# Moving the weight buffers of a one-core transformer block by 64 bytes, and spacing the gated MLP's activations 1040 bytes apart

## The chip, the core and the metric

The kernel runs on one core of a Trainium2 chip. The metric is the device time of one execution in microseconds (us); shorter is better. Three runs of the kernel before gave 1280.26, 1278.90 and 1280.11 us, median 1280.11.

## What is computed

One layer of a hybrid encoder block on a sequence of 256 tokens of width 2048, in float32:

```
mod = silu(c) @ W_ada + b_ada                  -> shift1, scale1, gate1, shift2, scale2, gate2
h   = RMSNorm(x) * (1 + scale1) + shift1
P   = h @ W_in                                 2048 -> 7184 columns
      group A: 4 heads x 256, bidirectional mLSTM;  group B: 8 heads x 128, 2-D neighbourhood attention
x   = x + gate1 * (concat[A, B] @ W_out)       2048 -> 2048
h   = RMSNorm(x) * (1 + scale2) + shift2
u, g = split(h @ W_up)                         2048 -> 2 x 5632
x   = x + gate2 * ((gelu(conv3(g)) * u) @ W_down)      5632 -> 2048
out = RMSNorm(x)
```

## The kernel before

Activations lie transposed: 128 features on the partitions, 256 tokens along the row. Every weight matrix is streamed once from HBM in pieces of 128 partitions x 1024 floats (4096 bytes a partition, tile `wr`; `wre` is two further buffers of it that serve only early on). float32 precision is had by splitting each operand in a high and a low part: ScalarE (ACT) casts `wr` to the high part `wh` (L356), VectorE (DVE) subtracts to get the low part `wl` (L364), and TensorE (PE) runs three matmuls for each 128x128 block of weights (`mm_w`, L391 to L393): high activation by high weight, low by high, high by low. In each, the activation row of 256 tokens is the moving operand (streamed through the array) and a 512-byte slice of `wh` or `wl` is the stationary one (loaded beforehand; the profile shows the loads as a row of its own, PEld). For the value projections (`mm_x`, L398 to L400) the sides change: 512 weight columns move and 128 tokens of an activation are loaded.

Stages in order of time:

- **Projections** (tile `acc`): 14 column chunks, five groups of K, with the modulation, the mLSTM and the attention beside them.
- **Output projection** (tile `acc_r`, activations `hh`/`hl`).
- **Up projection** (tile `acc_u`, `second_half`): 22 chunks of 512 columns x 16 K tiles x 4 column blocks x 3 matmuls = 4224 matmuls on `hh`/`hl`.
- **Down projection** (tile `acc_r` again, through `rows`): 44 K tiles x 16 column blocks x 3 = 2112 matmuls. The first 40 K tiles (j = 0 to 39) come from `aTh` and `aTl`, the last four from `hh`/`hl`.

The order of issue on every engine is fixed when the program is built, by a small model of the engines' times; addresses play no part in it.

What the change touches is where tiles lie. A pool lays its tiles one after another along the partition's row, in the order of first use, and pools follow each other: `cpool` (constants, `xT`), `ring` (`hh`, `hl`: 16 buffers of 1024 bytes each), `wpool` (`wr`, `h_t`, `wh`, `wl`, then `ared`, a tile of 16 bytes that takes 64, then `ar`), and after them, once the first half is over, `upool` (`aTh`, `aTl`, `g_c`). The start addresses within a partition that follow, and their place within 512 bytes, the size of a weight slice:

```
tile      before    mod 512     after    mod 512    step from buffer to buffer, before / after
hh         45568        0       45568        0      1024 / 1024
hl         61952        0       61952        0      1024 / 1024
wr         78336        0       78400       64      4096 / 4096
wh         97792        0       97856       64      4096 / 4096
wl        110080        0      110144       64      4096 / 4096
ar        122432       64      122496      128      4096 / 4096
aTh[0]    138816       64      138880      128      1024 / 1040
aTl[0]    179776       64      180480      256      1024 / 1040
wre       204640      352      204704      416      4096 / 4096
```

So before the change `hh` and `hl` stand at the same place within 512 bytes as every weight slice, and `aTh` and `aTl` stand 64 bytes past it, because of `ared`.

Of the kernel before, what the change touches and what calls it, by code (L numbers as in the profile page):

```python
# [7 lines left out]
F32 = mybir.dt.float32  # L8
F32R = mybir.dt.float32r
# [5 lines left out]
P = 128  # L15
D = 2048
KT = D // P
S = 256
# [8 lines left out]
FT = FF // P  # L27
# [40 lines left out]
N_LATE = 2.0  # L68
SEEDS = (0, 1, 1, 1, 1)
CH = 512  # L70
PIECE = 1024

CHUNK_COLS = {}
# [14 lines left out]
def splits(n, step):  # L88
    return [(a, min(a + step, n)) for a in range(0, n, step)]


def group_bounds():
    out, k = [], 0
    for g in KGROUPS:
        out.append((k, k + g))
        k += g
    return out
# [6 lines left out]
def up_order():  # L104
    return [(kind, c) for c in range(FF // CH) for kind in "gu"]

# [36 lines left out]
def block_kernel(ctx, tc, xT_d, cols_d, bg_d, rpb_d, ada_d, win_d, wg_d, wout_d, wup_d, wdown_d, const_d, out_d):  # L143
# [4 lines left out]
    cpool = ctx.enter_context(tc.tile_pool(name="cpool", bufs=1))  # L148
    ring = ctx.enter_context(tc.tile_pool(name="ring", bufs=1))
    wpool = ctx.enter_context(tc.tile_pool(name="wpool", bufs=1))  # L150
    psk = ctx.enter_context(tc.tile_pool(name="psk", bufs=2, space=PSUM))

    A.preload_act_table_set("natural_log_exp_and_others")
# [13 lines left out]
    def col(name):  # L167
        a, b = NCOL[name]
        return cols[:, a:b]

# [1 line left out]
    class Sched:  # L172
        LAT = {"PE": 0.2, "DVE": 0.14, "ACT": 0.14, "SP": 0.0, "POOL": 0.0}

# [69 lines left out]
    def held(what):  # L244
        return any(a in flags and b not in flags and what in c for a, b, c in HOLDS)
# [4 lines left out]
    def dve(n, *conds):  # L250
        return "DVE", 0.07 + n / 960, conds

    def act(n, *conds):
        return "ACT", 0.1 + n / 1210, conds
# [22 lines left out]
    class Ring:  # L277
# [12 lines left out]
        def take(self):  # L290
# [3 lines left out]
            if e:  # L294
                t = pools["e"].tile([P, PIECE], F32, name=self.tag + "e", tag=self.tag + "e", bufs=self.ne)
            else:
                t = wpool.tile([P, PIECE], F32, name=self.tag, tag=self.tag, bufs=self.n)
            return t, slots
# [19 lines left out]
        hl = ring.tile([P, S], F32R, name="hl", tag="hl", bufs=HH_BUFS)  # L318
        return hh, hl

# [1 line left out]
    class Stream:  # L322
        def __init__(self):
            self.todo, self.raw, self.cut, self.half = [], {}, {}, {}
# [4 lines left out]
        def add(self, src, nk):  # L329
            a = self.at.get(id(src), 0)  # L330
            self.at[id(src)] = a + P * nk * CH
            self.todo.append((src, a, nk))

        def view(self, t, nk):
            return t[:, : nk * CH].rearrange("p (a b) -> p a b", a=nk)

# [5 lines left out]
        def fetch(self, i, t):  # L342
            src, a, nk = self.todo[i]
            raw, slots = self.wr.take()
            n = nk * CH
            nc.sync.dma_start(raw[:, :n], src[a : a + P * n].rearrange("(p n) -> p n", p=P))
            self.raw[i] = (raw, sch.dma(t, n), slots)

        def cutting(self):
            for i, (_, _, nk) in enumerate(self.todo):  # L350
                n = nk * CH
                t = yield act(n, lambda: self.raw[i][1] if i in self.raw else None, self.wh.has())
                self.wh.take()
                raw = self.view(self.raw[i][0], nk)
                wh = self.view(wpool.tile([P, PIECE], F32R, name="wh", tag="wh", bufs=WH_BUFS), nk)
                A.copy(wh, raw)  # L356
                self.half[i] = (raw, wh, t)

        def rest(self):
            for i, (_, _, nk) in enumerate(self.todo):  # L360
                t = yield dve(nk * CH, lambda: self.half[i][2] if i in self.half and not held("r") else None)
                raw, wh, _ = self.half.pop(i)
                wl = self.view(wpool.tile([P, PIECE], F32R, name="wl", tag="wl", bufs=WH_BUFS), nk)
                V.tensor_sub(wl, raw, wh.bitcast(F32))  # L364
# [20 lines left out]
    stream = Stream()  # L385
# [50 lines left out]
        out[k] = (hh, hl)  # L436
        flags["h", part, k] = t

# [1 line left out]
    class Ada:  # L440
        def __init__(self):
            self.seq = ada_seq()
# [17 lines left out]
        def fetch(self, q, n, raw, slots, t):  # L460
            a = n * P * PIECE
            q.dma_start(raw, ada_d[a : a + P * PIECE].rearrange("(p n) -> p n", p=P))  # L462
            self.raw[n] = (raw, sch.dma(t, PIECE), slots)
# [145 lines left out]
    V.memset(ones, 1.0)  # L609
    V.memset(eps, EPS)  # L610

# [1 line left out]
    def silu():  # L613
        c = col("c")
        warm = kb.take()
        for i in range(WARM):
            T.matmul(warm[:, :P], ones, ones, start=i == 0, stop=i == WARM - 1)
        kb.give(5.3)
        sch.clock["PE"] = 1.1 + 0.215 * 2 * WARM
        yield act(16, lambda: 3.3)  # L620
        A.activation(small, c, AF.Exp, scale=-1.0)
        yield dve(1)
        V.tensor_scalar(small, small, 1.0, None, ALU.add)
        yield dve(100)
        V.reciprocal(small, small)
        t = yield dve(16)
        V.tensor_mul(sc, small, c)
        flags["sc"] = t
        diag = res["qb"].rearrange("p a b -> p (a b)")
        for q in range(4):  # L630
            d = diag[:, q * 512 : (q + 1) * 512]
            t = yield dve(512)
            V.tensor_tensor(d.rearrange("p (a b) -> p a b", a=4), ident.unsqueeze(1).to_broadcast([P, 4, P]),
                            sc[:, 4 * q : 4 * q + 4].unsqueeze(2).to_broadcast([P, 4, P]), ALU.mult)
            sch.add(srow_part(q, d), -2, t)

    def srow_part(q, d):
        yield pe(0.87, pb.has())
        tp = pb.take()
        T.matmul(tp, ones, d, start=True, stop=True)  # L640
        t = yield copy(512)
        put(srow[:, q * 512 : (q + 1) * 512], tp)
        pb.give(t)
        flags["srow", q] = t

# [1 line left out]
    ssb = {}  # L647

    n1_sums = KT - len(N1_PAIRS)
# [45 lines left out]

    mix = [None] * KT

# [1 line left out]
    nraw, nsl, npt = Slots(2), Slots(2), Slots(2)  # L699

    def natten(heads):
# [57 lines left out]
            mix[8 + h] = (hh, hl)  # L759
            flags["mix", 8 + h] = t  # L760

# [1 line left out]
    gst = {}  # L763
    mhs, mes = Slots(2), Slots(4)

# [243 lines left out]
            A.activation(o, o, AF.Exp, scale=-1.0)  # L1009
            flags["sig", i] = t  # L1010

# [1 line left out]
    bounds = group_bounds()  # L1013
    hT = [None] * KT

# [82 lines left out]
        stream.add(wout_d, (n1 - n0) * P * nk // CH)  # L1098
    at_up = len(stream.todo)

# [1 line left out]
    ss2 = {}  # L1102

    def wout_close(acc, c, n0, n1):
# [34 lines left out]
    order = up_order()  # L1139
# [4 lines left out]
    for _, n0, n1, _, nk in down_steps():  # L1144
        stream.add(wdown_d, (n1 - n0) * P * nk // CH)

# [1 line left out]
    for what in FIRST_LOADS:  # L1148
        if what == "x":
            a = 4 * len(xhere)  # L1150
# [7 lines left out]
            spare = spare.rearrange("p a b c -> p (a b c)" if len(spare.shape) == 4 else "p a b -> p (a b)")  # L1158
            ada.fetch(nc.sync, n, spare[:, n % 2 * PIECE : (n % 2 + 1) * PIECE], Slots(0), 0.0)

# [1 line left out]
    starts = [len(CHUNK_ORDER) * sum(len(splits(q1 - q0, 2)) for q0, q1 in bounds[:g]) for g in range(len(bounds))]  # L1162

    def pace(p):
# [23 lines left out]
    A.preload_act_table_set("gelu_and_others")  # L1188
    pstack.close()

# [1 line left out]
    upool = ctx.enter_context(tc.tile_pool(name="upool", bufs=1))  # L1192
    accu = ctx.enter_context(tc.tile_pool(name="accu", bufs=3, space=PSUM))
    aslots, gslots = Slots(3), Slots(GC_BUFS)
    h2 = [None] * KT
    n_own = FT - CH // P
    aTh = upool.tile([P, n_own, S], F32R, name="aTh")
    aTl = upool.tile([P, n_own, S], F32R, name="aTl")
    aT = [(aTh[:, j, :], aTl[:, j, :]) for j in range(n_own)] + [None] * (FT - n_own)
    cw0, cb0 = NCOL["cw"][0], NCOL["cb"][0]  # L1200
    gated = {}

# [35 lines left out]
        gslots.give(t)  # L1238
        flags["a", j] = t

# [1 line left out]
    ss3 = {}  # L1242
    gf0 = NCOL["gf"][0]

# [183 lines left out]
```

## Time and profile before

| what | value |
|---|---|
| median of the runs | 1280.11 us (1278.90 to 1280.26) |
| profiled execution, first to last instruction | 1278.2 us |
| PE busy | 1253.4 us, 98% |
| DVE, ACT, POOL busy | 908.2, 680.4, 110.6 us |
| moved by DMA | 322.55 MB, mean 252 GB/s |
| projections / output projection | from 19.4 us / from 395 us |
| up / down projection | from 504 us / 1014 to 1264 us |

The profile's own time for its execution is its span, 1278.2 us; the runs' times are the device's and lie 0.7 to 2.1 us above it. A matmul's own duration (0.28 us) is longer than the distance from its start to the next one's start, since matmuls overlap in the array; what sets the time is the distance between starts.

### The profile page before, as it was taken

To read this page: it belongs to the slowest core of one execution; us is meant where nothing else is said; L and a number is where in the kernel's file an instruction comes from. 1 tells how busy PE (TensorE), PEld (TensorE's weight loads), DVE (VectorE), ACT (ScalarE), POOL (GpSimd) and SP (SyncE) were. 2 spreads that over 40 slices of the span, in tenths; PEclk is the share of its full clock that TensorE was granted. 3 is DMA by queue.
4 is the path that set the end of the run, shared out by engine and by line. 5 is a ranking of instruction groups with operands and counts; after the bars stand their busy time and mean duration, and the time that the engine had idled before them with its cause. 6 is when DMAs were issued, how large, how long until landed. Compare 5 with 4: busy or idle time off the path is not lost.

```text
span 1278.2 us, 24381 instructions
## 1 busy us (share of the span) xinstructions
PE 1253.4 (98%) x9822; PEld 1217.2 (95%) x9822; DVE 908.2 (71%) x1382; ACT 680.4 (53%) x1027; POOL 110.6 (9%) x208
## 2 busy tenths in 40 slices
PE   8999999999999998999999999999999999999996
PEld 6889999999989998999999999999999999999995
DVE  5998879889999997997666666666665645454543
ACT  5986667668767444554444444444443534343442
POOL 1111111123112111010000000000000000000000
PEclk8999999999999998999999999999999999999998
DMA  9999889988888996786667666666655555655552
GB/s 322 408 370 352 298 297 374 338 285 292 298 297 277 376 330 244 263 323 235 217 215 228 217 216 215 224 224 220 202 184 183 182 183 184 193 183 186 185 182 91
DMA packets 91313, 322.55 MB, mean 252 GB/s; under 512 B 10560, under 2 KB 11072, under 8 KB 91200
## 3 DMA queue, kind: packets, MB, share of 16 engines
q1 hardware_dynamic: 63360, 220.84, 50.4%
q0 software_dynamic: 27840, 100.15, 23.3%
q8 instruction: 77, 1.26, 0.4%
q14 instruction: 36, 0.29, 0.1%
HBM read 318.85 MB, written 2.10 MB: 251 GB/s over the span
## 4 chain that ended last, share of the span: by engine, by line
PE 95%; ACT 3%; DVE 1%; DMA 1%; issue 0%; DVEq 0%; POOL 0%
PE acc_u L392 13%; PE acc_u L393 13%; PE acc_u L391 13%; PE acc_r L391 9%; PE acc_r L393 9%; PE acc_r L392 9%; PE acc L391 6%; PE acc L392 6%; PE acc L393 6%; PE acc L398 2%; PE acc L399 2%; PE acc L400 2%; ACT wh L356 1%; PE bank L890 1%; DMA n_raw<-in_rpb 1%; PE bank L850 1%
## 5 line engine op out<-in xcount | busy, mean ns | idle before, releaser
L364 DVE TENSOR_TENSOR wl<-wr,wh 128x1024 fp32r<-128x1024 f32 (+1 forms) x391 | 466.4, 1193 | 292.0 <-ACT wh L356 290.3
L356 ACT CAST wh<-wr 128x1024 fp32r<-128x1024 f32 (+1 forms) x391 | 400.4, 1024 | 467.1 <-PE acc_u L392 221.0
L391 PE MATMUL acc_u<-hh,wh 128*128 128x256 f32 x1408 | 399.8, 284 | 3.4 <-ACT hh L432 3.4
L392 PE MATMUL acc_u<-hl,wh 128*128 128x256 f32 x1408 | 399.7, 284 | 0.1
L393 PE MATMUL acc_u<-hh,wl 128*128 128x256 f32 x1408 | 399.5, 284 | 0.0
L391 PEld LDWEIGHTS acc_u<-hh,wh 128*128 128x128 f32 x1408 | 271.5, 193 | 3.9 <-ACT hh L432 3.9
L392 PEld LDWEIGHTS acc_u<-hl,wh 128*128 128x128 f32 x1408 | 271.5, 193 | 0.4 <-DVE hl L434 0.4
L393 PEld LDWEIGHTS acc_u<-hh,wl 128*128 128x128 f32 x1408 | 271.5, 193 | 0.0
L391 PE MATMUL acc<-hh,wh 128*128 128x256 f32 x640 | 186.8, 292 | 4.6 <-ACT hh L432 2.3
L392 PE MATMUL acc<-hl,wh 128*128 128x256 f32 x640 | 182.2, 285 | 0.0
L393 PE MATMUL acc<-hh,wl 128*128 128x256 f32 x640 | 182.0, 284 | 0.0
L391 PE MATMUL acc_r<-aTh,wh 128*128 128x256 f32 x640 | 179.7, 281 | 0.0
L392 PE MATMUL acc_r<-aTl,wh 128*128 128x256 f32 x640 | 178.6, 279 | 0.0
L393 PE MATMUL acc_r<-aTh,wl 128*128 128x256 f32 x640 | 178.6, 279 | 0.0
L462 POOL DMA_DIRECT2D ar<-in_ada x173 | 91.7, 531 | 716.4 <-DVE modp L489 352.5
L391 PEld LDWEIGHTS acc<-hh,wh 128*128 128x128 f32 x640 | 123.5, 193 | 10.0 <-ACT acc L260 3.6
L392 PEld LDWEIGHTS acc<-hl,wh 128*128 128x128 f32 x640 | 123.6, 193 | 1.0 <-DVE are L457 0.2
L393 PEld LDWEIGHTS acc<-hh,wl 128*128 128x128 f32 x640 | 123.6, 193 | 0.0
L393 PEld LDWEIGHTS acc_r<-aTh,wl 128*128 128x128 f32 x640 | 120.2, 188 | 0.0
L391 PEld LDWEIGHTS acc_r<-aTh,wh 128*128 128x128 f32 x640 | 120.1, 188 | 0.1
L392 PEld LDWEIGHTS acc_r<-aTl,wh 128*128 128x128 f32 x640 | 119.8, 187 | 0.1
L489 DVE CUSTOM_DVE_ANT_0 ar<-ar,srow,modp 128x1024 f32<-128x1024 f32 x87 | 111.1, 1277 | 0.6 <-DMA ar<-in_ada 0.3
(202 smaller groups left out, 1572.1 us busy)
## 6 DMA issues: line engine op xcount, KB each, us to landing
wr<-in_wup SPq DMA_DIRECT2D x176, 512.0 KB, 3.6
ar<-in_ada POOLq DMA_DIRECT2D x173, 512.0 KB, 5.6
wr<-in_wdown SPq DMA_DIRECT2D x88, 512.0 KB, 4.1
wr<-in_win SPq DMA_DIRECT2D x73, 512.0 KB, 5.7
wr<-in_wout SPq DMA_DIRECT2D x32, 512.0 KB, 5.8
wre<-in_win SPq DMA_DIRECT2D x25, 512.0 KB, 5.4
are<-in_ada POOLq DMA_DIRECT2D x15, 512.0 KB, 5.8
wr<-in_win SPq DMA_DIRECT2D x22, 256.0 KB, 5.4
```

The source lines that it names most:

```text
L356: A.copy(wh, raw)
L364: V.tensor_sub(wl, raw, wh.bitcast(F32))
L391: T.matmul(acc[:, n, :], w_h, h[0], start=st, stop=False, skip_group_check=True)
L392: T.matmul(acc[:, n, :], w_h, h[1], start=False, stop=False, skip_group_check=True)
L393: T.matmul(acc[:, n, :], w_l, h[0], start=False, stop=last, skip_group_check=True)
L398: T.matmul(acc[:, t, :], h_h, wh[:, k, :], start=first, stop=False, skip_group_check=True)
L399: T.matmul(acc[:, t, :], h_h, wl[:, k, :], start=False, stop=False, skip_group_check=True)
L400: T.matmul(acc[:, t, :], h_l, wh[:, k, :], start=False, stop=last, skip_group_check=True)
L462: q.dma_start(raw, ada_d[a : a + P * PIECE].rearrange("(p n) -> p n", p=P))
L489: V.tensor_tensor_reduce(raw, raw, srow[:, h * PIECE : (h + 1) * PIECE], 1.0, modp[:, part, k : k + 1] if h else cols[:, c : c + 1], ALU.m ...
L850: T.matmul(sp[:, u * S : (u + 1) * S], kT[:, 2 * h + k, u * P : (u + 1) * P], qT[:, 2 * h + k, :], start=k == 0, stop=k == 1)
L890: T.matmul(nu[1][:, : DH_A + 1], at[d][:, j, :], va[:, u, h, :], start=n == 0, stop=n == len(blocks) - 1)
```

## The change

Two constants are added. `SHIFT = 16` floats is an unused tile of 64 bytes a partition at the head of `wpool`, so that all of `wpool` and all that lies behind it stands 64 bytes further on, while `cpool` and `ring` stay. `STEP = 4` floats lengthens each row of `aTh` and `aTl` from 1024 to 1040 bytes; the last 16 bytes are not used. No instruction, no order and no wait differs on any engine; addresses do. (The diff also empties comment lines, left out here.)

```diff
 CH = 512
+SHIFT = 16
+STEP = 4
 PIECE = 1024
...
     wpool = ctx.enter_context(tc.tile_pool(name="wpool", bufs=1))
+    wpool.tile([P, SHIFT], F32, name="shift", tag="shift")
     psk = ctx.enter_context(tc.tile_pool(name="psk", bufs=2, space=PSUM))
...
     n_own = FT - CH // P
-    aTh = upool.tile([P, n_own, S], F32R, name="aTh")
-    aTl = upool.tile([P, n_own, S], F32R, name="aTl")
-    aT = [(aTh[:, j, :], aTl[:, j, :]) for j in range(n_own)] + [None] * (FT - n_own)
+    aTh = upool.tile([P, n_own, S + STEP], F32R, name="aTh")
+    aTl = upool.tile([P, n_own, S + STEP], F32R, name="aTl")
+    aT = [(aTh[:, j, :S], aTl[:, j, :S]) for j in range(n_own)] + [None] * (FT - n_own)
```

## The prediction

> **What bounds the kernel now.** I read the page first, then busy time by stage, then single matmuls.
>
> ```profile
> span 1278.2 us, 24381 instructions
> ...
> PE 1253.4 (98%) x9822; PEld 1217.2 (95%) x9822; DVE 908.2 (71%) x1382; ACT 680.4 (53%) x1027; POOL 110.6 (9%) x208
> ```
>
> PE is busy for all but 25 us of the span. By stage (length, busy time and count of each engine, granted clock, DMA share, GB/s):
>
> ```profile
> 0.00:100.00 100.00, 92.79 (x606) 80.44 (x607) 83.86 (x149) 77.73 (x137) 16.69 (x35) 0.97 0.97 367
> 100.00:200.00 100.00, 100.00 (x707) 93.91 (x706) 85.29 (x115) 67.60 (x100) 13.73 (x26) 1.00 0.90 316
> ...
> 395.00:498.00 103.00, 102.52 (x826) 101.08 (x825) 92.78 (x154) 48.65 (x75) 18.85 (x35) 1.00 0.93 331
> ...
> 520.00:1000.00 480.00, 480.00 (x4003) 480.00 (x4001) 323.76 (x433) 224.32 (x302) 19.53 (x37) 1.00 0.68 224
> 1014.00:1260.00 246.00, 246.00 (x2083) 245.84 (x2082) 117.65 (x119) 101.28 (x118) 0.00 (x0) 1.00 0.56 178
> ```
>
> From 100 us on PE has no gap to speak of, at full clock, and in the up and down projections the others have room. The two engines that feed it wait for it to free a weight buffer (us in total, times, longest):
>
> ```profile
> ACT wh L356 <- PE acc_u L392: 221.0, 142, 5.0
> ACT wh L356 <- PE acc_r L392: 182.0, 106, 3.5
> ```
>
> So the time is a count of matmuls times the distance between their starts, and that distance is not the same in the two last stages. A matmul takes 0.28 us, so a window also counts those begun 0.28 us before it: up 480.28/4003 = 120.0 ns, down 246.28/2083 = 118.2 ns, for the same instruction at the same clock. One place of the down projection shows both, where K tile 43 (`hh`, `hl`) gives way to K tile 0 of the next chunk (`aTh`, `aTl`). Timeline of PE: start, length, instruction.
>
> ```profile
> 1074.78 0.28 PE L391 MATMUL acc_r<-hh,wh 128*128 128x256 f32 x1
> ...
> 1076.22 0.28 PE L391 MATMUL acc_r<-aTh,wh 128*128 128x256 f32 x1
> ...
> 1081.88 0.28 PE L391 MATMUL acc_r<-aTh,wh 128*128 128x256 f32 x1
> ```
>
> Three matmuls a block, four blocks a K tile: 12 intervals on `hh` take 1.44 us, 120.0 ns each; the 48 on `aTh` take 5.66 us, 117.9 ns each. Same stage, same weight buffers, same shape; only the activations' place differs, level with the weight slice within 512 bytes for `hh`, 64 bytes past it for `aTh`. The load of the next weights starts together with each matmul (all engines' timeline):
>
> ```profile
> 1076.22 0.28 PE L391 MATMUL acc_r<-aTh,wh 128*128 128x256 f32 x1
> 1076.22 0.19 PEld L392 LDWEIGHTS acc_r<-aTl,wh 128*128 128x128 f32 x1
> ```
>
> It is longer, 192 ns for 188, where the places are level (groups of loads in the down stage: count, busy time, mean):
>
> ```profile
> L393 PEld LDWEIGHTS acc_r<-aTh,wl 128*128 128x128 f32 x640 | 120.2, 188 | 0.0
> ...
> L391 PEld LDWEIGHTS acc_r<-hh,wh 128*128 128x128 f32 x64 | 12.3, 192 | 0.0
> ```
>
> My reading: moving operand and next load, begun together at level addresses, get in each other's way once a matmul, at 120.0 - 117.8 = 2.2 ns. The 117.8 is from a stretch of PE in the down projection with no `hh` in it, 40.28/342:
>
> ```profile
> 1020.00:1060.00 40.00, 40.00 (x342) 1.00 0.57 186
> ```
>
> In the 480 us of the up projection every pair of buffers and slices occurs, some 512 bytes apart within 1024, and the distance stays 120.0; so 512 bytes apart is still level.
>
> **The change, part by part.** The 64 bytes make every `hh`/`hl` matmul unlevel. The counts, by form:
>
> ```profile
> L391 PE MATMUL acc_u<-hh,wh 128*128 128x256 f32 x1408 | 399.8, 284 | 3.4 <-ACT hh L432 3.4
> ...
> L391 PE MATMUL acc<-hh,wh 128*128 128x256 f32 x640 | 186.8, 292 | 4.6 <-ACT hh L432 2.3 <-ACT acc L260 1.6 <-ACT r_oa L260 0.3
> ...
> L391 PE MATMUL acc_r<-aTh,wh 128*128 128x256 f32 x640 | 179.7, 281 | 0.0
> ...
> L391 PE MATMUL acc_r<-hh,wh 128*128 128x256 f32 x320 | 92.1, 288 | 0.0
> ```
>
> Each row stands for three (L391 to L393). Up: 4224 x 2.2 ns = 9.3 us. Output projection: (320 - 64) x 3 = 768, 1.7 us. Down, its `hh` tiles: 64 x 3 = 192, 0.4 us. Projections: 1920, of which the first 100 us hold 3 x 143:
>
> ```profile
> L391 PE MATMUL acc<-hh,wh 128*128 128x256 f32 x143 | 43.1, 302 | 4.6 <-ACT hh L432 2.3 <-ACT acc L260 1.6 <-ACT r_oa L260 0.3
> ```
>
> The 1491 behind them are worth 3.3 us. Before 100 us PE stands for 7.2 us and DMA is at 0.97, so what PE gains there partly turns into waiting for ACT or the weights; of 429 x 2.2 = 0.9 us I keep half, 0.5 us. What hides the feeders elsewhere: a piece lasts 24 matmuls, 2.83 us after the change, and DVE's part of it is 1.2 us; DMA in the up stage goes from 0.68 to 0.69. Between 100 and 498 us DMA stands at 0.90 to 0.93; if that cover were gone, the 3.3 and 1.7 us would go with it.
>
> `mm_x` changes sides: after the change the loaded activation stands 64 bytes before the moving weights. Before, it was level:
>
> ```profile
> 150.14 0.39 PE L398 MATMUL acc<-wh,hh 128*128 128x512 f32 x1
> ...
> 150.82 0.39 PE L398 MATMUL acc<-wh,hh 128*128 128x512 f32 x1
> ```
>
> ```profile
> L399 PEld LDWEIGHTS acc<-wl,hh 128*128 128x128 f32 x128 | 24.2, 189 | 4.2
> ```
>
> 0.68 us for three, 226.7 ns each: the second 256 columns cost 106.7 ns, and the rest, 13.3 ns, is what a level matmul of 256 has too (120.0 - 106.7). Whether 2.2 of it go is not shown: between 0 and 384 x 2.2 = 0.8 us. Its loads take 189 ns already, as in the unlevel rows, so I take 0.
>
> The 1040-byte step changes 1920 matmuls that are unlevel already. Now the weights at 64 face `aTh` at 128 + 16 j and `aTl` at 256 + 16 j. With a period of 512 only `aTh[28]` (32 matmuls) and `aTl[20]` (16) are level: 0.1 us lost; all of them level would be 1920 x 2.2 = 4.2 us. The other end, a gain, is bounded by the gate's matmuls, whose loads are only 16 columns and at changing places:
>
> ```profile
> 252.02 0.28 PE L1023 MATMUL bank<-hh,wgh 128*16 128x256 f32 x1
> ...
> 253.55 0.28 PE L1024 MATMUL bank<-hh,wgl 128*16 128x256 f32 x1
> ```
>
> 13 intervals in 1.53 us, 117.7 ns: even a short load buys no more than `aTh` has. Read to 0.01 us at both ends that is 117.7 +- 0.8, so at best 0.8 ns on 8600 matmuls (all but the first 100 us), 6.9 us more. I take 0 for the step. A row that starts at a multiple of 16 bytes and no more costs nothing that a row shows: the float32 matmuls on `r_va`, whose rows are 1028 bytes, against those on `r_ka` with 1024 (chain of waits):
>
> ```profile
> 314.23 1.73 PE bank L850 x8
> ...
> 328.59 2.60 PE bank L890 x12
> ```
>
> 216.3 ns for 256 columns, 216.7 for 257.
>
> DMA writes `wr` 64 bytes further on. Landing times before, of a level buffer and of two that are not (`ar` at 64, `wre` at 96 past a multiple of 256):
>
> ```profile
> ar<-in_ada POOLq DMA_DIRECT2D x173, 512.0 KB, 5.6
> ...
> wr<-in_win SPq DMA_DIRECT2D x73, 512.0 KB, 5.7
> ...
> wre<-in_win SPq DMA_DIRECT2D x25, 512.0 KB, 5.4
> ```
>
> No slower; cost 0. The Trainium skill, "DMA: Bandwidth & Descriptors", section "How a descriptor splits into AXI transactions", has it that a descriptor not starting on 256 bytes also pays for the bytes back to that boundary; an estimate from its 32-byte beats is 130 for 128 on 4096 bytes, 1.6%, which on half the traffic of the first 100 us would be 0.8 us. These rows don't agree with it for a buffer in SBUF, as a write.
>
> Sum: 9.3 + 1.7 + 3.3 + 0.5 + 0.4 = 15.2 us, span 1278.2 - 15.2 = 1263.0. The median of the runs lies 1.9 us above this profile's span, so 1264.9: **1265 us**.
>
> **Rivals.** *Only one side of level is good.* `aTh` proves a load that starts 64 bytes behind the moving row; with `hh` the weights will start 64 bytes ahead. The loads of 16 and of 128 columns differ by 193 - 95 = 98 ns, so a full one reads for about 112 ns, as long as a matmul:
>
> ```profile
> L391 PEld LDWEIGHTS acc_u<-hh,wh 128*128 128x128 f32 x1408 | 271.5, 193 | 3.9 <-ACT hh L432 3.9
> ...
> L1023 PEld LDWEIGHTS bank<-hh,wgh 128*16 128x16 f32 x16 | 1.5, 95 | 0.3
> ```
>
> It reads 512 bytes while the row moves 1024, so a load behind falls further behind, and a load ahead is overtaken within the matmul. If that costs the same 2.2 ns, the gain is 0, and the step loses 0.1 us, or 0.5 with a period of 128, by which five rows of the forty are level (240 x 2.2): 1280 to 1281. For it: no row has weights ahead. Against: a load 64 bytes behind also falls back through a whole 512 by the matmul's end, and pays nothing for that.
>
> *No effect at all.* The change of pace at 1076.22 may belong to the buffers in another way than by address. The Trainium skill, "TensorE: Matmul & The Clock Gate", section "Step-by-step: what each phase is for", says that loading the next weights does not take read bandwidth from the running matmul, as the two have ports of their own; by that rule addresses could not matter. 120.0 against 117.9 ns within one stage disagrees. Time: 1280.
>
> *Half of it*, if overtaking costs about 1 ns: 7.6 us, 1272.5, or with the down stage turned level by a shorter period, 1265 + 4.2 = 1269.
>
> *Slower: overtaking stops both.* If meeting in mid-stream holds the row and the load one after the other, 4.4 ns in place of 2.2, it decides on the 7100 `hh` matmuls with weights ahead: +15.6 us, 1296. For it: nothing before tests it. Against: level starts, the worst case for meeting, cost only 2.2.
>
> **How the numbers follow.** Forecast 0.62 (1258 to 1269), half 0.10, no change or one side only 0.18, slower 0.10. The low end is 1265 less the 6.9 us of the gate's bound, the high end takes in no change with a little lost, 1281: without the cases at 1280 too little would be held. A measurement of this kernel can tell some 0.2%, 2.6 us, from no change. Faster 0.72, same 0.18, slower 0.10.
>
> **What would show it.** In the profile after: up 117.8 ns between starts in place of 120.0 (480 us holding 4077 matmuls), loads on `hh` at 188 in place of 193, down starting some 14.8 us earlier (9.3 + 1.7 + 3.3 + 0.5) and lasting as long as now. Wrong would be: up still at 120.0 (one side only), above it (overtaking), down no longer at 118, or PE gaps between 100 and 498 us (DMA or DVE late).

## The result, and the profile after

The change brought the median from 1279.51 to 1237.81 us: ratio 0.9669, 95% interval 0.9655 to 0.9683, 3.3% less time. The forecast was 1265 and the range ended at 1258: the right way, and not nearly far enough. One of the four executions of the changed kernel took 1256.67 us and is not in the ratio; the experiments come back to it.

The profiled execution of the changed kernel took 1235.8 us from first to last instruction, 42.4 less than before. Its page (in its kernel the lines of `mm_w` are L394 to L396):

```profile
span 1235.8 us, 24381 instructions
...
PE 1208.4 (98%) x9822; PEld 1171.7 (95%) x9822; DVE 906.3 (73%) x1382; ACT 682.9 (55%) x1027; POOL 110.5 (9%) x208
```

The same instructions, PE busy to the same 98%, and 45 us less of it. Where they went, by the first and last matmul of each stage in the two timelines:

| stage | before | after | less |
|---|---|---|---|
| projections | 375.2 us | 367.0 us | 8.2 us |
| output projection | 103.0 us | 97.6 us | 5.4 us |
| pause for the second norm | 6.2 us | 6.2 us | 0 |
| up projection | 509.7 us | 481.2 us | 28.6 us |
| down projection | 250.4 us | 249.5 us | 0.9 us |

The projections begin 0.6 us later than before. Busy time of PE in stretches of the up and of the down projection (length, busy time and count, clock, DMA share, GB/s):

```profile
520.00:960.00 440.00, 440.00 (x3885) 1.00 0.72 237
980.00:1025.00 45.00, 45.00 (x384) 1.00 0.58 185
```

With the 0.28 us of matmuls under way at the start of each, up now runs at 440.28/3885 = 113.3 ns from start to start, where it ran at 120.0 and I had said 117.8. Down on `aTh` and `aTl` runs at 45.28/384 = 117.9, as before. The timeline of PE in the up projection shows the steps one by one:

```profile
699.99 0.28 PE L394 MATMUL acc_u<-hh,wh 128*128 128x256 f32 x1
700.10 0.28 PE L395 MATMUL acc_u<-hl,wh 128*128 128x256 f32 x1
700.22 0.28 PE L396 MATMUL acc_u<-hh,wl 128*128 128x256 f32 x1
700.33 0.28 PE L394 MATMUL acc_u<-hh,wh 128*128 128x256 f32 x1
...
700.89 0.28 PE L396 MATMUL acc_u<-hh,wl 128*128 128x256 f32 x1
```

Eight distances in 0.90 us. The loads have shrunk from 193 to 188 ns, what the loads beside `aTh` had already:

```profile
L394 PEld LDWEIGHTS acc_u<-hh,wh 128*128 128x128 f32 x1408 | 265.2, 188 | 3.9 <-ACT hh L435 3.9
```

So a load of 188 ns goes with 117.8 and with 113.3: here it tells the level place from the others, not the two paces apart. The DMA engines are hardly held longer for the weights' new place; the queue that carries them held them for 52.3% of 1235.8 us, 646 us, against 50.4% of 1278.2, 644 us:

```profile
q1 hardware_dynamic: 63360, 220.84, 52.3%
```

From issue to landing a piece of `in_win` now takes 6.3 us, where it took 5.7. Whether that comes from the place or from the same bytes being asked for in less time is not shown.

In the projections PE waits more early on. Stages of the changed kernel, all engines in the order PE, PEld, DVE, ACT, POOL:

```profile
0.00:100.00 100.00, 89.71 (x601) 77.04 (x602) 83.33 (x147) 76.91 (x136) 16.66 (x35) 0.98 0.96 363
100.00:200.00 100.00, 100.00 (x737) 93.77 (x736) 88.45 (x121) 70.17 (x104) 14.25 (x27) 1.00 0.93 331
```

PE stands for 10.3 us of the first 100, 3.1 more than before, with DMA at 0.96; behind that it is without a gap again, 737 matmuls in 100 us for 707. The cover between 100 and 498 us held.

### The profile page after: what moved, and what is told of

The parts are those of the page before. It is cut to its first block, busy times and chain, and to the rows that moved or that the text cites. A ratio compares the mean times of both kernels' runs of the same rounds, so it can differ in the third digit from the quotient of the medians.

```text
span 1235.8 us, 24381 instructions
## 1 busy us (share of the span) xinstructions
PE 1208.4 (98%) x9822; PEld 1171.7 (95%) x9822; DVE 906.3 (73%) x1382; ACT 682.9 (55%) x1027; POOL 110.5 (9%) x208
## 3 DMA queue, kind: packets, MB, share of 16 engines
q1 hardware_dynamic: 63360, 220.84, 52.3%
## 4 chain that ended last, share of the span: by engine, by line
PE 93%; DMA 3%; ACT 2%; DVE 1%; SPq 0%; issue 0%; DVEq 0%; ACTq 0%
PE acc_u L395 13%; PE acc_u L396 13%; PE acc_u L394 13%; PE acc_r L395 9%; PE acc_r L394 9%; PE acc_r L396 9%; PE acc L394 5%; PE acc L395 5%; PE acc L396 5%; PE acc L403 2%; PE acc L402 2%; PE acc L401 2%; DMA wre<-in_win 2%; PE bank L893 1%; ACT wh L359 1%; DMA wr<-in_win 1%
## 5 line engine op out<-in xcount | busy, mean ns | idle before, releaser
L394 PE MATMUL acc_u<-hh,wh 128*128 128x256 f32 x1408 | 389.8, 277 | 3.4 <-ACT hh L435 3.4
L395 PE MATMUL acc_u<-hl,wh 128*128 128x256 f32 x1408 | 389.7, 277 | 0.1
L396 PE MATMUL acc_u<-hh,wl 128*128 128x256 f32 x1408 | 389.4, 277 | 0.0
L394 PEld LDWEIGHTS acc_u<-hh,wh 128*128 128x128 f32 x1408 | 265.2, 188 | 3.9 <-ACT hh L435 3.9
L395 PEld LDWEIGHTS acc_u<-hl,wh 128*128 128x128 f32 x1408 | 265.2, 188 | 0.4 <-DVE hl L437 0.4
L396 PEld LDWEIGHTS acc_u<-hh,wl 128*128 128x128 f32 x1408 | 265.2, 188 | 0.0
L394 PE MATMUL acc<-hh,wh 128*128 128x256 f32 x640 | 182.9, 286 | 6.8 <-ACT hh L435 2.3
L394 PE MATMUL acc_r<-aTh,wh 128*128 128x256 f32 x640 | 180.2, 282 | 0.0
L396 PE MATMUL acc_r<-aTh,wl 128*128 128x256 f32 x640 | 179.4, 280 | 0.0
L395 PE MATMUL acc<-hl,wh 128*128 128x256 f32 x640 | 178.1, 278 | 0.1
L396 PE MATMUL acc<-hh,wl 128*128 128x256 f32 x640 | 178.0, 278 | 0.0
L394 PEld LDWEIGHTS acc<-hh,wh 128*128 128x128 f32 x640 | 121.0, 189 | 12.4 <-ACT acc L263 4.3
L395 PEld LDWEIGHTS acc<-hl,wh 128*128 128x128 f32 x640 | 121.0, 189 | 1.1 <-DVE are L460 0.3
L396 PEld LDWEIGHTS acc<-hh,wl 128*128 128x128 f32 x640 | 121.1, 189 | 0.0
L395 PEld LDWEIGHTS acc_r<-aTl,wh 128*128 128x128 f32 x640 | 120.5, 188 | 0.1
L396 PEld LDWEIGHTS acc_r<-aTh,wl 128*128 128x128 f32 x640 | 120.6, 188 | 0.0
L394 PEld LDWEIGHTS acc_r<-aTh,wh 128*128 128x128 f32 x640 | 120.4, 188 | 0.1
```

What stands on the lines that cost most here:

```text
L394: T.matmul(acc[:, n, :], w_h, h[0], start=st, stop=False, skip_group_check=True)
L395: T.matmul(acc[:, n, :], w_h, h[1], start=False, stop=False, skip_group_check=True)
L396: T.matmul(acc[:, n, :], w_l, h[0], start=False, stop=last, skip_group_check=True)
```

## The experiments

Theory A at the start: the distance from the place of the moving row to the place of the next matmul's weights, within a slice, sets the pace. Level is 120.0 ns, weights 64 bytes behind 117.8, weights 64 bytes ahead 113.3. "Ahead" and "behind" below are of the weights, seen from the activations. Every pace is a window's length plus 0.28 us over its count.

### Each half of the change alone, and a level down projection

```diff
 SHIFT = 16
-STEP = 4
+STEP = 0
```

> SHIFT = 16 as in the change, STEP = 0: aTh and aTl are back at 1024 bytes a row, all at 64 bytes past the weights' place within 512. Theory A (the distance between the start of the loaded weights and that of the moving row, taken within 512 bytes, sets the pace: 120.0 ns level, 117.8 with weights 64 behind, 113.3 with weights 64 ahead): up stays at 113.3 ns, down goes back to 117.8 (before: 250.4 us from its first to its last matmul), so within 2 us of the change: 1236 to 1239. Theory B (the 1040-byte rows carry part of the gain, in some way not seen in the spacing): over 1245.

Measured: 1238.04 us, ratio 0.9673 (0.9657 to 0.9690), the same as the whole change within the intervals. Up 113.3, down 117.9:

```profile
520.00:960.00 440.00, 440.00 (x3885) 1.00 0.71 237
980.00:1025.00 45.00, 45.00 (x384) 1.00 0.59 186
```

```diff
-    wpool.tile([P, SHIFT], F32, name="shift", tag="shift")
```

> SHIFT tile left out, STEP = 4: only the rows of aTh and aTl are 1040 bytes. Theory A: projections and up as before at 120.0 ns, down around 118 as in the change: 1278 to 1281, no change. Theory B: under 1270.

Measured: 1280.10 us, ratio 0.9999 (0.9990 to 1.0009). Up 480.28/4003 = 120.0, down 46.28/392 = 118.1:

```profile
520.00:1000.00 480.00, 480.00 (x4003) 1.00 0.68 224
1022.00:1068.00 46.00, 46.00 (x392) 1.00 0.58 189
```

The 64 bytes are the whole change; the rows 1040 bytes apart do nothing that can be measured in the time.

```diff
-STEP = 4
+STEP = 0
+PAD = 96
...
     upool = ctx.enter_context(tc.tile_pool(name="upool", bufs=1))
+    upool.tile([P, PAD], F32, name="pad", tag="pad")
```

> SHIFT = 16, STEP = 0, and an unused tile of 384 bytes at the head of upool, so that aTh and aTl stand at 0 within 512 like hh and hl, and the weights are 64 bytes ahead of them too. Theory A: the down projection also runs at 113.3 ns, 2112 x 4.6 ns = 9.7 us less than the change: 1227 to 1230. Theory C (the gain hangs on where the weights lie, or on hh and hl, not on the distance between the two): down stays at 117 to 118 ns, 1236 to 1239.

Measured: 1228.77 us, ratio 0.9597 (0.9581 to 0.9613), better than the change by 9 us. The down projection has followed, 170.28/1502 = 113.4 ns:

```profile
520.00:960.00 440.00, 440.00 (x3885) 1.00 0.71 237
980.00:1150.00 170.00, 170.00 (x1502) 1.00 0.61 194
```

The weights lie where they lay in the change, and `aTh` and `aTl` were moved under them: it is the distance between the two, and theory C falls. One of four executions took 1256.56.

### Which distances

In three runs the two stages were given two distances each, with `SHIFT` for the up and `PAD` for the down projection. These three kernels, and the three that follow up to the end of the next section, were executed once each; the kernel before took 1281.78 us beside four of them and 1283.77 beside the other two.

```diff
-SHIFT = 16
-STEP = 4
+SHIFT = 8
+STEP = 0
+PAD = 88
```

> Weights 32 bytes ahead of hh and hl (SHIFT = 8), 96 ahead of aTh and aTl (padding of 352 bytes, STEP = 0). Theory D (64 ahead is one good place among bad ones; all others give 117 to 120): up 117 to 120, down 117 to 119: 1255 to 1275. Theory E (any distance ahead that stays the same from matmul to matmul gives 113; the rows 1040 bytes apart are at 118 because the distance keeps changing): both 113 to 114, 1228.

> Weights 128 bytes ahead of hh and hl, 256 ahead of aTh and aTl. Theory D: 117 to 120 in both stages, 1255 to 1275. Theory E: 113 to 114 in both, 1228.

 (`SHIFT = 32`, `PAD = 48`)

> Weights 192 bytes ahead of hh and hl, 32 behind aTh and aTl. Theory D: 117 to 120 in both stages, 1255 to 1275. Theory E: up 113 to 114, down 117 to 118 as with 64 behind: 1237.

 (`SHIFT = 48`, `PAD = 120`)

| ahead, bytes | pace, ns | stage and run |
|---|---|---|
| 0 | 120.0 | up, before |
| 32 | 118.3 | up, 1271.03 us |
| 96 | 117.3 in the first chunk, 118.7 in the next two | down, same run |
| 128 | 118.7 | up, 1276.94 us |
| 256 | 120.0 | down, same run |
| 192 | 117.8 | up, 1267.92 us |
| -32 | 120.0 in the first chunk, 116.7 in the next two | down, same run |

The paces of the down projection are averages over the 40 K tiles of a chunk that come from `aTh` and `aTl`, taken from the starts in the timeline; the last four K tiles, on `hh` and `hl`, stand at the up projection's distance and are left out. The rows behind the second and the third run, up (470.28/3963, 470.28/3993) and down; a short window is good to some 0.2 ns:

```profile
520.00:990.00 470.00, 470.00 (x3963) 1.00 0.69 227
1012.00:1057.00 45.00, 45.00 (x377) 1.00 0.57 179
```

```profile
520.00:990.00 470.00, 470.00 (x3993) 1.00 0.70 228
...
1010.00:1058.00 48.00, 48.00 (x403) 1.00 0.58 186
1070.00:1115.00 45.00, 45.00 (x388) 1.00 0.62 188
```

Theory D had it: of these distances none reaches 113.3. And 256 is level again, so the period seems to be 256 bytes and not the 512 of the prediction; 192 is then the same as 64 behind, and has its 117.8. Two distances, 96 and -32, changed pace from the first chunk to the second with nothing moved. And one place of the third run does not fit at all. In its down projection the last four K tiles come from `hh` and `hl`, at the same 192 bytes as in its up projection:

```profile
1061.21 0.28 PE L395 MATMUL acc_r<-hh,wh 128*128 128x256 f32 x1
...
1066.65 0.28 PE L395 MATMUL acc_r<-aTh,wh 128*128 128x256 f32 x1
```

48 distances in 5.44 us, 113.3 ns: the same distance, two paces.

The period was tried by itself, with two more distances near 64 (`SHIFT = 80`, `PAD = 96`, or 16 and 88, with the rows of `aTh` and `aTl` moved by 16 bytes inside a longer tile):

> Weights 320 bytes ahead of hh and hl (64 more than 256), 48 ahead of aTh and aTl. The run with 256 ahead in the down projection had 120.0 ns like the level one, so the period seems to be 256, not 512 as the prediction took it. If it is: up at 113.3 ns. If 64 ahead is good only by itself: up at 117 to 120. Down, 48 ahead: between the 118.3 of 32 and the 113.3 of 64 if the good place is broad (114 to 116), 117 to 119 if it is narrow. Time 1237 to 1240 with a period of 256, over 1255 without.

> Weights 64 bytes ahead of hh and hl, 80 ahead of aTh and aTl. Up 113.3 as before. Down 114 to 116 if the good place is broad, 117 to 119 if it is narrow (96 ahead gave 118.2): 1232 to 1240.

The first took 1240.58 us: up, 320 ahead, 440.28/3884 = 113.4, as a period of 256 has it; down, 48 ahead, 119.2 on `aTh` and `aTl`. The second took 1258.30 us, above its forecast of 1232 to 1240: down, 80 ahead, 119.2, and up, 64 ahead as in the change, 460.28/3908 = 117.8:

```profile
520.00:980.00 460.00, 460.00 (x3908) 1.00 0.69 228
```

The good place is narrow, and it isn't always good: with the same distance as in the change the whole up projection stayed at 117.8 to its end, though the output projection before it, at that distance too, took the change's 97.6 us. One load in three is longer in that stage, 192 ns, the other two 188:

```profile
L397 PEld LDWEIGHTS acc_u<-hh,wl 128*128 128x128 f32 x1408 | 271.0, 192 | 0.0
L395 PEld LDWEIGHTS acc_u<-hh,wh 128*128 128x128 f32 x1408 | 265.1, 188 | 3.9 <-ACT hh L436 3.9
```

That broke theory A as I had it. Even the run with `SHIFT` alone, whose four executions agree, has both paces on `hh` at 64 ahead in one trace: the four K tiles at the end of the first chunk of the down projection, and those halfway through its last one:

```profile
1029.37 0.28 PE L394 MATMUL acc_r<-hh,wh 128*128 128x256 f32 x1
...
1034.81 0.28 PE L394 MATMUL acc_r<-aTh,wh 128*128 128x256 f32 x1
```

```profile
1187.47 0.28 PE L394 MATMUL acc_r<-hh,wh 128*128 128x256 f32 x1
...
1190.29 0.28 PE L394 MATMUL acc_r<-aTh,wh 128*128 128x256 f32 x1
```

48 distances in 5.44 us are 113.3 ns each, 24 in 2.82 us are 117.5.

### Which pair of operands

```diff
+    ring2 = ctx.enter_context(tc.tile_pool(name="ring2", bufs=1))
+    ring2.tile([P, 16], F32, name="shift", tag="shift")
...
-        hl = ring.tile([P, S], F32R, name="hl", tag="hl", bufs=HH_BUFS)
+        hl = ring2.tile([P, S], F32R, name="hl", tag="hl", bufs=HH_BUFS)
```

(No `SHIFT` tile in `wpool`; `STEP = 0`, `PAD = 96`.)

> The 64-byte tile stands between the buffers of hh and those of hl: hh at 0, hl at 64, the weights at 64; aTh and aTl at 0, both 64 before the weights. Which pair of operands matters? If it is the moving row and the load that runs beside it (the NEXT matmul's weights), then in the up projection the distance from the start of a matmul on hl to the next start is 120 ns and that from the two on hh 113 (mean 115.5). If it is a matmul's row and its OWN weights, the distance that ends with the start of a matmul on hl is the long one. If it is the step from one moving row to the next, both distances beside hl change and neither has 120.0 or 113.3. Down at 113.4 as in the run with level aTh. Time by either of the first two: 1228.8 + 4224 x 2.2 ns + 4 = 1242.

Measured: 1259.67 us for the 1242 expected; up 470.28/3992 = 117.8, down 113.2. Averaged over the up projection's timeline, the distance that begins with a matmul on `hl` is 120.0 ns, those that begin with the two on `hh` are 117.1 and 116.2. There the longest is where the first answer had it, beside the load that is level with `hl`; but the 113 of the other two did not come. And it is not there in every stage: in the output projection of the same trace, from 400 to 495 us, the distances without a wait average 120.5 ns from a matmul on `hh` and `wh`, 119.0 from one on `hl` and 117.6 from the third. So which pair matters stays open; 117 ns on `hh` with weights 64 ahead may be the slower pace that the run with 80 ahead has shown, or an effect of the neighbours.

### Two paces at one distance

Theory S: at 64 and at 192 bytes the stream of loads and rows has two steady paces, 117.8 and 113.3, and keeps the one into which it falls. The next three kernels were executed four times each.

> Weights 192 bytes ahead of hh and hl (64 behind, with the period of 256), 64 ahead of aTh and aTl, STEP = 0. Two runs so far had 64 ahead in the up projection and came out at 113.3 and 117.8 ns from the stage's start to its end, and in one run hh at 192 ran at 113.5 in the down projection and at 117.8 in the up projection. Theory S (at 64 and at 192 bytes there are two steady paces, 113.3 and 117.8, and how the stage is entered decides which): here the up projection is at 117.8 or at 113.3 from end to end, by execution; times near 1256 or, less 4224 x 4.5 ns = 19 us, near 1237, and another 9 us higher where the down projection is at 117.8. Theory F (192 is at 117.8 for ever, 64 at 113.3, and the run at 117.8 was disturbed): all executions within 3 us of each other, up at 117.8.

 (`SHIFT = 48`, `STEP = 0`, `PAD = 96`)

Measured: four executions, 1256.68, 1265.44, 1265.11 and 1241.86 us: far more than 3 us apart, and theory F falls. The profiled one, the first, had 460.28/3908 = 117.8 in the up projection throughout, and 45.28/399 = 113.5 in the down projection on `aTh` and `aTl`:

```profile
520.00:980.00 460.00, 460.00 (x3908) 1.00 0.70 229
1005.00:1050.00 45.00, 45.00 (x399) 1.00 0.60 191
```

The two at 1265 lie 9 us above it, what 1920 matmuls of the down projection at 117.8 would add (8.6 us); the one at 1241.86 lies 15 below, of the 19 that an up projection at 113.3 from end to end would save. Those three have no trace, so that their stages ran so is not shown.

```diff
+    upool.tile([P, 56], F32, name="pad", tag="pad")
+    pools["kick"] = [upool.tile([P, S], F32R, name=n, tag=n) for n in ("kh", "kl")]
+    upool.tile([P, 40], F32, name="pad2", tag="pad2")
...
         hh, hl = hl_tiles()
+        if part and k == KT - 1:
+            hh, hl = pools["kick"]
```

> As the run with 192 and 64, but K tile 15 of the up projection has its activations in a place of their own, 32 bytes past the weights' place, so that every chunk of columns ends with 12 matmuls at another distance. Theory S: after that other distance the stream falls into the fast pace, as it did in the down projection of the run with 32 behind: up at 113.3 to 114 for 15 of 16 K tiles and about 118 for the sixteenth, from the end of the first chunk on, whatever the start was: 1232 to 1240. Theory F: up stays at 117.8: 1250 or more.

Measured: 1243.13 us (1241.91, 1243.85, 1258.13, 1242.40), ratio 0.9742 (0.9685 to 0.9798). The profiled execution, up projection, in three stretches: before the first K tile 15, between the third and the fourth, and over the rest:

```profile
510.00:550.00 40.00, 40.00 (x342) 1.00 0.83 298
572.00:590.00 18.00, 18.00 (x161) 1.00 0.76 251
600.00:980.00 380.00, 380.00 (x3348) 1.00 0.68 222
```

40.28/342 = 117.8, then 18.28/161 = 113.5, then 380.28/3348 = 113.6 with the twelve matmuls at another distance in every chunk. The same buffers, the same distance, one stage: the pace changed when the stream had gone through another distance. It took two passes: behind the first K tile 15 the stream was still at 117.8, behind the second and all later ones at 113.3. The time forecast, 1232 to 1240, forgot that projections and output projection are at 192 too and have no such K tile: the output projection ran at 117.7. Why one execution took 1258 is not known; if its up projection stayed at 117.8, theory S's "whatever the start was" is too strong.

> Weights 64 bytes ahead of hh, hl, aTh and aTl as in the run with level padding (1228.8), and K tile 15 of the up projection 32 bytes past the weights' place. Theory S: no execution can stay at 117.8 in the up or the down projection; 352 x 12 / 16 matmuls at about 118 in place of 113.3 cost 1.2 us and the return to the pace as much again: all executions between 1228 and 1234. Theory F: as the run without it but 1 to 3 us longer, 1229 to 1232, with the same chance of an execution near 1256.

 (as the run before, with `SHIFT = 16`)

Measured: 1229.26 us, ratio 0.9606 (0.9591 to 0.9621), the four between 1227.94 and 1230.58. Up 440.28/3874 = 113.6, down 113.4:

```profile
520.00:960.00 440.00, 440.00 (x3874) 1.00 0.71 237
980.00:1150.00 170.00, 170.00 (x1502) 1.00 0.60 193
```

As fast as the level padding, and no execution near 1256. That four without one show little: at the rate met so far with 64 ahead, one execution in four or five, four in a row without one come three to four times in ten.

With theory S the sizes of two executions without a trace come out: an up projection at 117.8 costs 4224 x 4.5 ns = 19.0 us, and the changed kernel's 1256.67 lies 19.1 above 1237.55, the median of its other three; with the down projection as well 28.5, and 1256.56 lies 28.8 above 1227.76, the same median of the level padding. That is a match in size, not shown: the 2688 matmuls of projections and output projection could give up to 12.1 us too, so other sums come near.

## Why the prediction was wrong

- **The bound was right.** The time is a count of matmuls times the distance between their starts, and PE kept no gap where I said it would keep none.
- **The mechanism was right in part.** The level place is slow, and moving the weights 64 bytes away from `hh` and `hl` ended it, in all three stages that use them. But level is only the slow end of a range: apart from the pace of 113.3, the other distances that were tried lie at 116.7 to 119.2 ns (-32 at 120.0 too). The 4.5 ns that make the gain large belong to something that the prediction did not have, a second, faster pace. That the first shift tried was one that can run at it was luck: with 32 bytes the up projection ran at 118.3, with 128 at 118.7, about what the prediction forecast. The Trainium skill has in "TensorE: Matmul & The Clock Gate", section "Step-by-step: what each phase is for", that loading the next weights takes no read bandwidth from the running matmul. One instruction at 120.0, 117.8 and 113.3 ns, by the address of the weights, does not fit a reading of this by which addresses cannot matter.
- **The step** was put at 0, and is at 0 in the time (0.9990 to 1.0009). The row of 216.3 ns that was to show this for 1024 bytes has `r_qa` moving; `r_ka` is the loaded one.
- **The size of a matmul's gain was the step that failed**: "120.0 - 117.8 = 2.2 ns" took the pace on `aTh` for what any matmul has that isn't level. It was 6.7. Up: 28.6 us for the 9.3 of the sum; output projection 5.4 for 1.7; projections 8.2 for 3.8. The pace on `aTh` was one of two that this distance has: the third run of distances shows 113.3 at the same 192 bytes.
- **The low end was a wrong bound.** I read "even a short load buys no more than `aTh` has" from the gate's matmuls at 252 us, 117.7 ns on average. Another group of the same matmuls, in the same trace before the change, goes faster:

```profile
172.02 0.28 PE L1024 MATMUL bank<-hh,wgl 128*16 128x256 f32 x1
...
172.47 0.28 PE L1025 MATMUL bank<-hl,wgh 128*16 128x256 f32 x1
```

Four distances in 0.45 us are 112.5 ns, read to 0.01 us. One group was no bound for the instruction, as one distance is none for the others. Why the two groups differ is not shown. The rows 1040 bytes apart show no good place either: in the first three chunks of the changed kernel's down projection the paces of single K tiles run from 116.9 to 119.2 ns, though at j = 8 and 24 the weights stand 64 bytes ahead of `aTh`.

- **The rival on the sign fell.** Weights ahead were not worse. Nor is it the sign: 192, which is 64 behind, ran at 113.3 too, and 64 ahead at 117.8. The argument set against it counted in slices of 512 bytes; the runs repeat with 256.
- **`mm_x`** was put at 0 of 0 to 0.8 us gain; by the timelines those of its distances in which PE did not wait, 370 of 384, average 229.1 ns after and 228.3 before: nothing was gained. That the 13.3 ns are shared with a level matmul of 256 columns was no finding, since 106.7 had been worked out by taking 120.0 off.
- **The first 100 us** were to give half of their share and gave nothing: 601 matmuls for 606, with 3.1 us more of standing.

## What to carry to other kernels

Where PE runs without a gap, the byte address of the loaded operand against that of the moving one can be a tuning parameter: a tile of 64 bytes in front of a pool took 3.3% off a tuned kernel, and the same place for the last stage's activations another 0.7%. Look for it where one instruction has two paces in one profile, and then try the distances, since a pace seen at one is no bound for the others. One profile of such a kernel may show one of two paces; several executions, and the pace by stage, tell more than the median.

## What the runs showed of the hardware that was not expected

- The pace of a 128x128 load with 256 float32 columns moving repeats with 256 bytes between the operands, as far as two pairs of distances show it: 120.0 ns at 0 and at 256; 113.3 at 64 and 113.4 at 320; at 32, 48, 80, 96 and 128 bytes 117.3 to 119.2.
- At 64 and 192 bytes there are two steady paces, 113.3 and 117.8 ns. An up projection, which begins after a pause, fell into one of them and kept it for 4224 matmuls in every trace in which the distance stayed the same; passing through another distance can change it. At 96 and at -32 (224) bytes too the traces have two paces, 117.3 and 118.7, 120.0 and 116.7. What fixes the choice, and why 64 bytes in particular, stays open: nothing here looks below a matmul.
